# Second feed-forward: chunks 5, 6 and 9, 10 in pairs with seven block products, weight blocks summed by accumulating transfers

## The chip, the cores and the metric

The kernel runs on one core of one Trainium2 chip. The metric is the device time of one execution in microseconds; the time of a kernel is the median of several runs. Before the change it is 784.1 us, the median of three runs between 783.6 and 784.39.

The engines are named as in the profile: PE (TensorE) multiplies matrices and loads its stationary operand with LDWEIGHTS (PEld), DVE (VectorE) and ACT (ScalarE) work on tiles, POOL (GpSimd) and SP (SyncE) here mainly issue transfers.

## The reference

One layer of a streaming encoder over 256 positions and a model width of 1024: a feed-forward, a mixing block, a memory attention, and a second feed-forward. The change is in the second feed-forward alone:

```python
def rmsnorm(x, g):
    y = x32 * lax.rsqrt(jnp.mean(x32 * x32, axis=-1, keepdims=True) + EPS)
    return (y * g.astype(jnp.float32)).astype(x.dtype)

def swiglu(h, w_in, w_down):
    gate, up = jnp.split(h @ w_in, 2, axis=-1)
    return (jax.nn.silu(gate) * up) @ w_down
...
        h = rmsnorm(x, ffn2_pre_g[l])
        x = x + 0.5 * rmsnorm(swiglu(h, ffn2_w_in[l], ffn2_w_down[l]), ffn2_post_g[l])
```

`w_in` is 1024 x 5632 (gate and up), `w_down` 2816 x 1024, all in float32.

## The kernel before

**Arithmetic.** Each float32 operand of a product is split into a high part rounded to float32r and the rest, hi and lo (`split`, `load_split`). A product is hi·hi + hi·lo + lo·hi, three matmuls for a block of 128 rows of the inner dimension. The inputs are kept transposed (inner dimension on the partitions), hi and lo side by side, in `X`, of class `Joined`.

**Weights.** A unit is a tile of 128 x 1024 float32 (512 KB): two blocks of 128 rows and 512 columns. `load_split` loads it from SP into a `raw` buffer (4 of them), copies it to `hi` on ACT and subtracts on DVE for `lo` (8 buffers each). So a unit is split as soon as the unit eight places ahead of it has been used by PE, and loaded as soon as a raw buffer has been split.

**Chunks.** The hidden width 2816 is cut into 11 chunks of 256. A chunk's input projection has 512 columns (gate and up), that is 4 units: units 0 and 1 are the first half of the inner dimension, 2 and 3 the second.

- By tokens (`act_tok`, chunks 0 and 1 of the second feed-forward): the inputs of 128 tokens are stationary, 512 weight columns move, 24 matmuls of 128x512 for each half of the tokens. The result has tokens on the partitions; `act_evac` applies the gate, and `flush` transposes it on PE (4 transposes of 128x128 for a pair of token halves and a chunk) and splits it into `acts`.
- By columns (`act_col`, chunks 2 to 10): 128 weight columns are stationary, the tokens' hi and lo (512 wide) move; the lo weights take the hi tokens alone (256 wide). That is 32 matmuls of 128x512 and 32 of 128x256 for a chunk, and the result is already transposed. `added` sums the two halves of a PSUM bank, with a copy on ACT and an addition on DVE.
- Down-projection (`down`): chunk c, token half h, 2 units, 12 matmuls of 128x512 into one of two pairs of PSUM banks that accumulate over all chunks (`accs`).

**Order.** The loop over chunks does a chunk's input projection and behind it the down-projection of an earlier chunk: chunk 2 with down-projection 0, and so on to chunk 8 with 6; chunk 9 has none, chunk 10 is followed by 7. The last three (8, 9, 10) come at the end, first token half first, followed by `post` (norm, gain, residual, store). Each engine runs its queue strictly in order; a scheduler has placed the instructions of DVE, ACT, PE, POOL and SP in advance, and `high_priority`, `issue_after` and `after` steer it. PSUM has 4 banks for `acc`, 2 for `mm`, 2 for `tr`. The pool `extra` has 4 buffers of 128 x 1024.

Of the kernel before, what the change touches and what calls it, by code (L numbers as in the profile page):

```python
# [11 lines left out]
F32 = mybir.dt.float32  # L12
F32R = mybir.dt.float32r
# [5 lines left out]
P = 128  # L19
# [12 lines left out]
SETS = ((0, 1), (2, 4), (8, 16), (32,), (64,), (128,))  # L32

STAG = 3

L_ACT = 21
L_F1 = 24
# [41 lines left out]
def block_kernel(ctx: ExitStack, tc: tile.TileContext, wts, head_in, gf_in, x_in, mem_in, memT_in, cols, rows, fbias, masks, out):  # L79
# [12 lines left out]
    def MM(*args, **kw):  # L92
        log.append(PE.matmul(*args, **kw).ins)  # L93
# [9 lines left out]
    def nm(s):  # L103
        count[0] += 1
        return f"{s}_{count[0]}"

    def m4(shape, dt=F32, n="m"):
        return mp.tile(shape, dt, tag="m4", name=nm(n))

    def s1(n=1, dt=F32, name="s"):  # L110
        return sp.tile([P, n], dt, tag=f"s{n}", name=nm(name), bufs=16)

    def acc():
        return pp.tile([P, 512], F32, tag="acc", name=nm("acc"), bufs=4)

    def mm():
        return pp.tile([P, 512], F32, tag="mm", name=nm("mm"), bufs=2)
# [13 lines left out]
    def parts_of():  # L131
        return [wp.tile([P, D], F32R, tag=t, name=nm(t), bufs=8) for t in ("hi", "lo")]
# [15 lines left out]
    def unit(name, i):  # L148
        u = _AT[name] + i
        if u not in cache:  # L150
            cache[u] = load_split(wts[u - 4], behind=hold.get(u), parts=place.get(u))
        return cache[u]
# [4 lines left out]
    def blk(units, kb, n=512):  # L157
        hi, lo = units[kb // 2]
        o = (kb % 2) * 512
        return hi[:, o : o + n], lo[:, o : o + n]  # L160

    def split(hi, lo, src):
        a = S.copy(hi, src)
        b = V.tensor_tensor(out=lo, in0=src, in1=hi.bitcast(F32), op=ALU.subtract)
        return a.ins, b.ins

    class Pair:
# [7 lines left out]
        def more(self):  # L175
            self.h.append(m4([P, 4, T], F32R, "hT"))
            self.l.append(m4([P, 4, T], F32R, "lT"))
# [65 lines left out]
    def bc(a, shape, dim):  # L243
        return a.unsqueeze(dim).to_broadcast(shape)
# [172 lines left out]
    def ffn(w_in, w_dn, X, r2, n_tok, i_row, first_half, second_half=None):  # L417
# [7 lines left out]
        def flush(n):  # L425

            if late:
                c = late.pop(0)
                tr = trp()
                trv = tr.rearrange("p (j t) -> p j t", j=2)  # L430
                with after(n):
                    for h in range(2):
                        for j in range(2):
                            PE.transpose(trv[:, j, h * P : (h + 1) * P], ats[c, h][:, j * P : (j + 1) * P], ident)  # L434
                    split(acts[c][:, 0], acts[c][:, 1], trv)

        def act_evac(ps, c, h):
            sg = sp.tile([P, FC], F32, tag="c1", name=nm("sg"), bufs=7)
            S.activation(sg, ps[:, :FC], AF.Silu, scale=r2[h])
            a = sp.tile([P, FC], F32, tag="c1", name=nm("at"), bufs=7)  # L440
            V.tensor_tensor(out=a, in0=ps[:, FC:], in1=sg, op=ALU.mult)
            ats[c, h] = a
            if h == 1:
                late.append(c)

        def act_tok(c, h):
            ps = mm()
# [35 lines left out]
        def down(c, h, cols=((0, 512), (512, 1024))):  # L483
            act = acts[c]
            hs = slice(h * P, (h + 1) * P)
            for j in range(2):
                wh, wl = unit(w_dn, 2 * c + j)
                ah, al = act[:, 0, j, hs], act[:, 1, j, hs]
                for lo, up in cols:
                    for i, (a, w) in enumerate(((ah, wh), (ah, wl), (al, wh))):  # L490
                        MM(accs[h][lo // 512][:, lo % 512 : lo % 512 + up - lo], a, w[:, lo:up], start=(c == 0 and j == 0 and i == 0), stop=(c == NFF - 1 and j == 1 and i == 2))

        for c in range(n_tok):
            acts[c] = m4([P, 2, 2, T], F32R, "act")
        for h in range(2):
# [8 lines left out]
        if callable(r2):  # L504
# [6 lines left out]
                    act_evac(outs[c][h], c, h)  # L511
            n_tok = 2
        for c in range(n_tok, NFF):
            acts[c] = m4([P, 2, 2, T], F32R, "act")
            if c == 2 and first_half:
                n = len(log)
                (outs,) = act_first((c,), mm)
                for h in range(2):
                    flush(n + L_ACT + 24 * h)
                    act_evac(outs[h], c, h)  # L520
            else:
                n = len(log)
                up = act_col(c)
                flush(n + L_ACT)
                flush(n + L_ACT + 20)
                split(acts[c][:, 0], acts[c][:, 1], up)
            if c == 6:
                grow = load_row(i_row)
                if first_half:
                    with tc.issue_after(loads[-1]):  # L530
                        nc.sync.dma_start(masks_s, masks)
            if accs is None:
                accs = [[acc(), acc()], [acc(), acc()]]

            while done < (NFF - STAG if c == NFF - 1 else min(c - 1, NFF - STAG - 1)):
                n = len(log)
                for h in range(2):
                    down(done, h)
                flush(n + L_ACT)
                done += 1  # L540
        left, right = (0, 512), (512, 1024)
# [836 lines left out]
```

## Time and profile before

| | |
|---|---|
| median of three runs | 784.1 us |
| span of the profiled execution | 782.4 us |
| second feed-forward's chunk 3 begins, by PE's timeline | 631.5 us |
| chunks 9 and 10 begin | 731.2 and 742.4 us |
| last matmul ends | 775.5 us |
| HBM read, written | 146.24 MB, 1.06 MB |

The profiled execution's own time is the span; the difference to the median of the runs is what lies around it. The profile gives starts and durations for each instruction. A matmul's duration overlaps with the next one, so that its cost is read from the distance between starts. "Idle before" is time in which an engine stood waiting, with what released it.

### The profile page before, as it was taken

The page shows a single profiled execution, that of the slowest core. Times are in us where ns is not written, and L with a number is a line of the kernel's source. Part 1 is how long each engine was busy: PE and PEld are TensorE (multiplying, and loading weights), DVE is VectorE, ACT ScalarE, POOL GpSimd, SP SyncE. Part 2 cuts the span into 40 slices and gives each one's busy share as a digit, 9 for nine tenths or more (in the row PEclk, how much of TensorE's full clock was granted, in tenths as well). Part 3 has the DMA queues.
Part 4 walks back from the last instruction along what each step waited for, and adds up shares of the span by engine and source line. Part 5 has one row for each costly group of instructions (what it writes and reads, how often), then busy time and mean ns, then how long its engine had stood idle before and what let it go on. Part 6 is the DMA issues. An engine that isn't in the chain of part 4 may idle for free.

```text
span 782.4 us, 12131 instructions
## 1 busy us (share of the span) xinstructions
PE 773.8 (99%) x4598; PEld 667.2 (85%) x4598; DVE 560.1 (72%) x907; ACT 467.2 (60%) x789; POOL 16.0 (2%) x39
## 2 busy tenths in 40 slices
PE   9999999999999999999999999999999999999996
PEld 7888888888888998898888888888888888888885
DVE  6766655586778999888776666885588566655663
ACT  7664544566765668567686345753667655544542
POOL 0000000000000101100000000000000000000000
PEclk9999999999999999999999999999999999999999
DMA  9766665464654545835576655465175556665431
GB/s 346 258 218 205 226 210 207 162 214 141 218 187 145 181 137 178 303 105 167 196 271 220 212 186 166 152 203 182 54 268 163 168 181 208 208 208 192 162 108 54
DMA packets 44506, 148.09 MB, mean 189 GB/s; under 512 B 5144, under 2 KB 8864, under 8 KB 44448
## 3 DMA queue, kind: packets, MB, share of 16 engines
q1 hardware_dynamic: 43168, 144.83, 54.4%
q0 software_dynamic: 848, 2.12, 1.0%
q8 instruction: 36, 0.59, 0.3%
q10 hardware_dynamic: 432, 0.37, 0.1%
q14 instruction: 22, 0.18, 0.1%
HBM read 146.24 MB, written 1.06 MB: 188 GB/s over the span
## 4 chain that ended last, share of the span: by engine, by line
PE 98%; DMA 1%; DVE 0%; ACT 0%; issue 0%; SPq 0%; DVEq 0%; ACTq 0%
PE mm L93 43%; PE acc L93 39%; PE tr L93 14%; PE tr L375 1%; DMA head<-in_head_dram 1%; PE tr L1015 0%; PE tr L434 0%; PE tr L1109 0%; PE acc L1228 0%; DVE xs L411 0%; DVE post L406 0%; ACT hi L590 0%; SPq L574 0%; ACT hlT L362 0%; SPq L569 0%
## 5 line engine op out<-in xcount | busy, mean ns | idle before, releaser
L145 DVE TENSOR_TENSOR lo<-raw,hi 128x1024 fp32r<-128x1024 f32 (+1 forms) x252 | 299.4, 1203 | 70.2 <-ACT hi L143 48.0
L143 ACT CAST hi<-raw 128x1024 fp32r<-128x1024 f32 (+1 forms) x252 | 254.8, 1037 | 68.5 <-DMA raw<-in_wts_dram 32.2
L93 PE MATMUL mm<-hi,hlT 128*128 128x512 f32 (+1 forms) x480 | 143.3, 378 | 0.0
L93 PE MATMUL acc<-hi,act 128*128 128x512 f32 x352 | 111.2, 390 | 0.0
L93 PEld LDWEIGHTS mm<-hi,hlT 128*128 128x128 f32 x480 | 88.3, 188 | 14.3
L93 PE MATMUL mm<-hlT,hi 128*128 128x512 f32 (+1 forms) x384 | 91.8, 374 | 0.0
L93 PE MATMUL mm<-lo,hlT 128*128 128x512 f32 (+1 forms) x240 | 89.4, 378 | 0.0
L93 PEld LDWEIGHTS mm<-hlT,hi 128*128 128x128 f32 x384 | 68.5, 189 | 11.1
L93 PEld LDWEIGHTS acc<-hi,act 128*128 128x128 f32 x352 | 66.2, 188 | 13.4
L93 PE MATMUL tr<-hlT,hi 128*128 128x512 f32 x304 | 76.1, 392 | 0.0
L93 PE MATMUL acc<-lo,act 128*128 128x512 f32 x176 | 68.8, 391 | 0.0
L93 PE MATMUL acc<-hlT,hi 128*128 128x512 f32 x272 | 68.4, 393 | 0.0
L93 PEld LDWEIGHTS tr<-hlT,hi 128*128 128x128 f32 x304 | 54.7, 189 | 9.8
L93 PEld LDWEIGHTS acc<-hlT,hi 128*128 128x128 f32 x272 | 48.9, 189 | 8.8
L93 PE MATMUL mm<-hlT,lo 128*128 128x256 f32 x352 | 54.6, 283 | 0.0
L93 PEld LDWEIGHTS mm<-hlT,lo 128*128 128x128 f32 x352 | 50.0, 190 | 3.3
L93 PEld LDWEIGHTS mm<-lo,hlT 128*128 128x128 f32 x240 | 45.0, 188 | 6.9
L215 ACT COPY plo<-mm 128x256 f32<-128x256 f32 x40 | 14.9, 372 | 48.9 <-PE mm L93 48.9
L93 PEld LDWEIGHTS tr<-hlT,lo 128*128 128x128 f32 x304 | 41.5, 190 | 3.0
L93 PE MATMUL tr<-hlT,lo 128*128 128x256 f32 x304 | 42.4, 282 | 0.0
L93 PEld LDWEIGHTS acc<-hlT,lo 128*128 128x128 f32 x272 | 37.3, 190 | 2.7
L93 PE MATMUL acc<-hlT,lo 128*128 128x256 f32 x272 | 38.6, 283 | 0.0
(256 smaller groups left out, 1008.9 us busy)
## 6 DMA issues: line engine op xcount, KB each, us to landing
raw<-in_wts_dram SPq DMA_DIRECT2D x247, 512.0 KB, 4.4
raw<-in_gf_dram SPq DMA_DIRECT2D x12, 344.0 KB, 3.8
head<-in_head_dram SPq DMA_DIRECT2D x7, 392.0 KB, 6.7
grow<-in_rows_dram SPq DMA_DIRECT2D x4, 512.0 KB, 6.7
xs<-in_x_dram SPq DMA_DIRECT2D x2, 512.0 KB, 7.8
cbm<-cd POOLq DMA_DIRECT2D x2, 512.0 KB, 7.6
brow<-in_rows_dram SPq DMA_DIRECT2D x4, 256.0 KB, 4.0
memT<-in_memT_dram SPq DMA_DIRECT2D x2, 512.0 KB, 5.3
```

Source lines behind the costliest of these rows:

```text
L93: log.append(PE.matmul(*args, **kw).ins)
L143: S.copy(h, r)
L145: V.tensor_tensor(out=l, in0=r, in1=h.bitcast(F32), op=ALU.subtract)
L215: S.copy(lo, ps[:, T:])
L375: PE.transpose(blocks[-1][1], src(kb), ident)
```

## The change

`PAIRS` names chunks that are computed together with the next one: 5 with 6 and 9 with 10 in the second feed-forward, none in the first. A pair is a product of the inputs (two halves of tokens by two halves of the inner dimension) and of the weights (two halves of the inner dimension by two chunks), both seen as 2 x 2 blocks. Instead of the eight products of blocks that this takes by tokens, it is put together from seven, by a scheme of Strassen's kind (Winograd's form): some products take sums and differences of input blocks and sums of weight blocks, and the results are combined by additions.

- `pair_inputs`, once, at chunk 2: the sums and differences of the input blocks on DVE, then split. Since the second half of the tokens has another norm factor than the first, its inputs are scaled by the ratio (`rho`), and `q` takes it out again.
- `sum_load`, `more`: sums of weight blocks. The first summand is loaded from SP into a buffer of pool `extra`, each further summand is added by a transfer from POOL with `accum_op`. One sum ("sums") is used as W00 + W01 and then, with W11 added, again; the other ("both") as W01 + W11 and then, with W00 and W10 added, again. The third and fourth summands can be added only when the first version has been split.
- `act_pair`: the seven products, 12 matmuls of 128x512 each, with waiting down-projections put between them by `step_between`; then the combinations on DVE, four calls of `act_evac`, and transposes by `flush`.
- `act_evac` can multiply by `q` and by another scale.
- The loop over chunks takes a pair as one step.

On the engines, after scheduling: in PE's queue the first pair has the halves of down-projections 3 and 4 between its products, one each after the first and second product, after b3 and after b4, and twelve matmuls of chunk 7 ahead of the pair's last product (that of e). The second pair has four matmuls of b3 ahead of the second product, and eleven of down-projection 7 ahead of its last product. ACT copies the new "sums" (first unit) ahead of `S.copy(p1, b0)` in the second pair, behind it in the first. POOL has twenty new transfers, SP eight new ones and four fewer plain units.

```diff
--- before.py
+++ after.py
+
+PAIRS = {"f1_in": (), "f2_in": (5, 9)}
 ...
-        def act_evac(ps, c, h):
+        def act_evac(ps, c, h, r=None, q=None):
             sg = sp.tile([P, FC], F32, tag="c1", name=nm("sg"), bufs=7)
-            S.activation(sg, ps[:, :FC], AF.Silu, scale=r2[h])
+            silu = S.activation(sg, ps[:, :FC], AF.Silu, scale=r2[h] if r is None else r).ins
             a = sp.tile([P, FC], F32, tag="c1", name=nm("at"), bufs=7)
-            V.tensor_tensor(out=a, in0=ps[:, FC:], in1=sg, op=ALU.mult)
+            if q is None:
+                V.tensor_tensor(out=a, in0=ps[:, FC:], in1=sg, op=ALU.mult)
+            else:
+                V.scalar_tensor_tensor(out=a, in0=ps[:, FC:], scalar=q, in1=sg, op0=ALU.mult, op1=ALU.mult)
             ats[c, h] = a
             if h == 1:
                 late.append(c)
+            return silu
 ...
+        def pair_inputs():
+            rho = sp.tile([P, P], F32, tag="c1", name=nm("rho"), bufs=7)
+            V.reciprocal(rho, row[:, :P])
+            V.tensor_tensor(out=rho, in0=row[:, P:], in1=rho, op=ALU.mult)
+            q = s1(name="q")
+            V.reciprocal(q, r2[1])
+            V.tensor_tensor(out=q, in0=r2[0], in1=q, op=ALU.mult)
+            xf = [m4([P, 4, T], n="xf") for _ in range(2)]
+            for k in range(2):
+                for i in range(2):
+                    x = X.t[2 * k + i].bitcast(F32)
+                    V.tensor_tensor(out=xf[k][:, 2 * i : 2 * i + 2], in0=x[:, :, 0], in1=x[:, :, 1], op=ALU.add)
+                V.tensor_tensor(out=xf[k][:, :, P:], in0=xf[k][:, :, P:], in1=bc(rho, [P, 4, P], 1), op=ALU.mult)
+            a, b, d, e = (xf[k][:, :, h * P : h * P + P] for h in range(2) for k in range(2))
+            ss = [m4([P, 2, 4, P], n="ss") for _ in range(2)]
+            de, aed, ad, baed = (t[:, i] for t in ss for i in range(2))
+            V.tensor_tensor(out=de, in0=d, in1=e, op=ALU.subtract)
+            V.tensor_tensor(out=aed, in0=a, in1=de, op=ALU.subtract)
+            V.tensor_tensor(out=ad, in0=a, in1=d, op=ALU.subtract)
+            V.tensor_tensor(out=baed, in0=b, in1=aed, op=ALU.subtract)
+            out = {}
+            for n, x in (("baed", baed), ("aed", aed), ("de", de), ("ad", ad), ("e", e)):
+                t = m4([P, 2, 4, P], F32R, "sx")
+                split(t[:, 0], t[:, 1], x)
+                out[n] = t
+            return out, q
+
+        def sum_load(c, n, halves):
+            t = []
+            for j in range(2):
+                r = wp.tile([P, D], F32, tag="extra", name=nm("sraw"), bufs=4)
+                more(r, c, *halves[0], j, None)
+                more(r, c, *halves[1], j, ALU.add)
+                t.append(r)
+            return t
+
+        def more(r, c, k, n, j, op):
+            src = wts[_AT[w_in] + 4 * (c + n) + 2 * k + j - 4]
+            if op is None:
+                loads.append(nc.sync.dma_start(r, src).ins)
+            else:
+                G.dma_start(r, src, accum_op=op)
+
+        def act_pair(c, between):
+            sx, q = pairs_in
+
+            def of(n):
+                return lambda kk: (sx[n][:, 0, kk], sx[n][:, 1, kk])
+
+            def of_x(k):
 ...
+            def splits(t):
+                u = []
+                for r in t:
+                    p = parts_of()
+                    split(p[0], p[1], r)
+                    u.append(p)
+                return u
+
+            def plain(k, n):
+                return [unit(w_in, 4 * (c + n) + 2 * k + j) for j in range(2)]
+
+            def product(ps, stat, u, start):
+                for kk in range(4):
+                    ah, al = stat(kk)
+                    wh, wl = blk(u, kk)
+                    for i, (x, y) in enumerate(((ah, wh), (ah, wl), (al, wh))):
+                        MM(ps, x, y, start=start and kk == 0 and i == 0, stop=kk == 3 and i == 2, skip_group_check=not start)
+
+            def step_between():
+                if between:
+                    between.pop(0)()
+
+            def half_tile(n):
+                return sp.tile([P, 512], F32, tag="z2", name=nm(n), bufs=3)
+
+            sums, both = sums_of_pair.pop(c)
+            b0 = mm()
+            product(b0, of_x(0), plain(0, 0), True)
+            vw = m4([P, 2, 512], n="vw")
+            pc = m4([P, 2, 512], n="pc")
+            p1, v, w = pc[:, 0], vw[:, 0], vw[:, 1]
+            S.copy(p1, b0)
+            step_between()
+            product(b0, of_x(1), plain(1, 0), False)
+            act_evac(b0, c, 0)
+            step_between()
+            b3 = mm()
+            u = splits(sums)
+            for j in range(2):
+                more(sums[j], c, 1, 1, j, ALU.add)
+            product(b3, of("de"), u, True)
+            step_between()
+            b4 = mm()
+            u = splits(both)
+            for k, n in ((0, 0), (1, 0)):
+                for j in range(2):
+                    more(both[j], c, k, n, j, ALU.add)
+            product(b4, of("ad"), u, True)
+            step_between()
+            b1 = trp()
+            product(b1, of("aed"), splits(sums), True)
+            with tc.high_priority():
+                V.tensor_tensor(out=v, in0=p1, in1=b1, op=ALU.subtract)
+                V.tensor_tensor(out=w, in0=b3, in1=v, op=ALU.subtract)
+                t = half_tile("c11")
+                V.tensor_tensor(out=t, in0=w, in1=b4, op=ALU.subtract)
+                act_evac(t, c + 1, 1, r2[0], q)
+            b2 = trp()
+            product(b2, of("baed"), plain(1, 1), True)
+            with tc.high_priority():
+                t = half_tile("c01")
+                V.tensor_tensor(out=t, in0=w, in1=b2, op=ALU.add)
+                act_evac(t, c + 1, 0)
+            step_between()
+            product(b4, of("e"), splits(both), False)
+            t = half_tile("c10")
+            V.tensor_tensor(out=t, in0=v, in1=b4, op=ALU.add)
+            silu = act_evac(t, c, 1, r2[0], q)
+            if c + 1 == NFF - 1:
+                table(silu)
+            while between:
+                step_between()
+
+        def pair_loads(c):
+            if c in pairs and c not in sums_of_pair:
+                sums_of_pair[c] = sum_load(c, 0, ((0, 0), (0, 1))), sum_load(c, 1, ((0, 1), (1, 1)))
+
+        sums_of_pair = {}
+        pairs, pairs_in = PAIRS[w_in], None
 ...
         for c in range(n_tok, NFF):
+            if c - 1 in pairs:
+                continue
+            if c > 2 and c not in pairs:
+                pair_loads(c + 1)
+            if c in pairs:
+                pair_loads(c)
             acts[c] = m4([P, 2, 2, T], F32R, "act")
-            if c == 2 and first_half:
+            if c in pairs:
+                acts[c + 1] = m4([P, 2, 2, T], F32R, "act")
+                downs = [(i, h) for i in range(done, min(c, NFF - STAG - 1)) for h in range(2)]
+                done = max(done, min(c, NFF - STAG - 1))
+
+                def one(i, h):
+                    n = len(log)
+                    down(i, h)
+                    if h == 1:
+                        flush(n + L_ACT - 12)
+
+                act_pair(c, [lambda i=i, h=h: one(i, h) for i, h in downs])
+            elif c == 2 and first_half:
 ...
-            if c == 6:
+            last = c + 1 if c in pairs else c
+            if c <= 6 <= last:
 ...
-
-            while done < (NFF - STAG if c == NFF - 1 else min(c - 1, NFF - STAG - 1)):
+            if c == 2 and pairs:
+                pairs_in = pair_inputs()
+
+            while done < (NFF - STAG if last == NFF - 1 else min(c - 1, NFF - STAG - 1)):
                 n = len(log)
                 for h in range(2):
                     down(done, h)
+                    if last > c:
+                        flush(n + 11)
+                        n = len(log)
                 flush(n + L_ACT)
                 done += 1
```

1 line of the change is left out of this document (added).

## The prediction

> **What bounds the kernel now.** I read the page's summary first, then its chain of waits, then the stretches of the second feed-forward by engine, and last the order of instructions there.
>
> ```profile
> span 782.4 us, 12131 instructions
> PE 773.8 (99%) x4598; PEld 667.2 (85%) x4598; DVE 560.1 (72%) x907; ACT 467.2 (60%) x789; POOL 16.0 (2%) x39
> PE 98%; DMA 1%; DVE 0%; ACT 0%; issue 0%; SPq 0%; DVEq 0%; ACTq 0%
> 681.37:697.99 16.62, 16.62 (x90) 14.34 (x89) 10.50 (x14) 8.54 (x13) 0.00 (x0) 1.00 0.55 193
> 714.60:731.21 16.61, 16.61 (x89) 14.34 (x88) 10.77 (x15) 8.91 (x13) 0.00 (x0) 1.00 0.56 199
> 731.21:753.53 22.32, 22.32 (x129) 19.66 (x128) 12.95 (x19) 12.16 (x20) 0.00 (x0) 1.00 0.57 189
> 753.53:782.40 28.87, 21.95 (x98) 17.84 (x96) 12.69 (x24) 7.80 (x19) 0.00 (x0) 0.94 0.11 37
> ```
>
> The chain that ended last is 98% PE, and in the last four rows (length; then PE, PEld, DVE, ACT, POOL busy; granted clock; DMA share; GB/s) PE never pauses before its last matmul at 775. So a PE microsecond saved or lost inside the stage moves the end. DVE is busy 10.5 of 16.6 us, the DMA engines 0.55 to 0.57 of the time. The stretches are chunk 6 (681.37), chunk 8 (714.60) and chunks 9 and 10 (731.21).
>
> **The change part by part.** *Products.* Pitches, from starts in PE's timeline:
>
> ```profile
> 614.05 1.98 PE L93 MATMUL mm<-hlT,hi 128*128 128x512 f32 x8
> 618.21 0.60 PE L434 MATMUL tr<-ident,at 128*128 128x128 f32 x4
> 626.07 0.40 PE L93 MATMUL acc<-hi,act 128*128 128x512 f32 x1
> ...
> 681.37 1.98 PE L93 MATMUL mm<-hlT,hi 128*128 128x512 f32 x8
> 692.52 0.40 PE L93 MATMUL acc<-hi,act 128*128 128x512 f32 x1
> 697.99 1.98 PE L93 MATMUL mm<-hlT,hi 128*128 128x512 f32 x8
> ```
>
> A chunk by columns takes 692.52 − 681.37 = 11.15 us; the 24 matmuls of a down-projection that follow take 5.47 us, 0.228 each. Two chunks: 22.30 us. A pair has 7 products of 12 matmuls of that same shape, 84 × 0.228 = 19.15 us. A pair must also transpose its activations, eight times, which columns don't need. Chunk 2 has eight such transposes among its matmuls and takes 626.07 − 614.05 = 12.02 us, so they cost 0.87 us. Net 22.30 − 19.15 − 0.87 = 2.28 us a pair, **4.6 us for both**, if PE never waits.
>
> *Vector work.* A pair splits 14 weight blocks instead of 8, and evacuates with five 512-wide and four 256-wide operations in place of the sums and the gate of two chunks. The inputs' sums (some 15 operations 512 wide) are made once, during chunks 2 and 3.
>
> ```profile
> L145 DVE TENSOR_TENSOR lo<-raw,hi 128x1024 fp32r<-128x1024 f32 x57 | 68.7, 1220 | 20.8 <-ACT hi L143 12.8 <-PE tr L93 7.8 <-ACT hlT L362 0.2
> L143 ACT CAST hi<-raw 128x1024 fp32r<-128x1024 f32 x57 | 58.0, 1049 | 11.1 <-DMA raw<-in_wts_dram 7.9 <-PE mm L93 2.3
> L466 DVE TENSOR_TENSOR up<-up,gate 128x512 f32<-128x512 f32 x9 | 6.2, 684 | 0.0
> L217 DVE TENSOR_TENSOR gate<-mm,plo 128x256 f32<-128x256 f32 x18 | 7.6, 422 | 17.5 <-ACT plo L215 17.5
> L163 ACT CAST act<-up 128x512 fp32r<-128x512 f32 x9 | 5.6, 622 | 15.9 <-DVE up L466 15.9
> ```
>
> Inputs: 15 × 0.68 = 10 us of DVE, against 16.6 − 10.5 = 6 us idle in each of two chunk periods: hidden, because what is pushed back there are down-projection blocks and the next chunk's first two blocks, split some 12 us ahead of use; 0 taken, 2 us if that lead is short. Pair: 14 splits of 1.14 us pitch (below) plus 5 us make 21 us against PE's 19.15 us (ACT: 14 × 1.05 and some 4 us of evacuations) and the down-projections among it. That fits on average; where it doesn't is a matter of waits.
>
> *Transfers.* A pair loads 6 plain blocks and 4 first summands from SP, and adds 10 further summands from POOL: 20 transfers of 512 KB instead of 8. No accumulating transfer is in the trace. Call X the time from its issue to its landing.
>
> ```profile
> q1 hardware_dynamic: 43168, 144.83, 54.4%
> raw<-in_wts_dram SPq DMA_DIRECT2D x247, 512.0 KB, 4.4
> cbm<-cd POOLq DMA_DIRECT2D x2, 512.0 KB, 7.6
> out_dram<-xs SPq DMA_DIRECT2D x1, 128.0 KB, 1.8
> rd<-runs POOLq DMA_DIRECT2D x4, 1.0 KB, 2.1
> DMA to landing us min/median/max: 3.2/4.5/7.6
> SPq L141 <- DVE lo L145: 85.7, 30, 8.5
> ```
>
> Bounds: 3.2 us (the fastest plain block of this stage, last row but one) and 7.6 us (a plain block from POOL, one row broadcast) + 1.5 us for reading the destination too (512 KB at 144.83 MB / (0.544 × 782.4 us) = 340 GB/s), 9.1 us. I take 4.7 us: the plain block's median plus the 0.3 us by which POOL's smallest transfer lands later than a small one of SP's. That says the destination's read hides beside that of HBM.
>
> On all 16 engines a plain block occupies 1.5 us by the row above. The Trainium skill (Collectives: The Full Stack, "The bandwidth ceiling: the fold count and why AG ≠ RS ≠ AR") says that an adding transfer is slow "because the add needs **two source reads**", half the rate of a copy; by it the block would occupy 3.1 us and X be 6.2, which by the sum below gives 784.9 us and, with transfers queueing, the slow rival. No run so far has such a transfer.
>
> *First pair* (PE starts it where chunk 5 starts, T0 = 664.76). Four half down-projections lie between its products, so PE reaches the end of the sixth product at 10 × 2.73 = 27.3 us. ACT and DVE are strict queues here. The second operand ("both") is read by 13.4 us, when its buffers come free at 9.6 and 10.9; then two summands go in one behind the other, each waiting for the one before: landed at 13.4 + 2X. Behind that wait ACT still copies 1.05 us of it and 1.05 us of chunk 7's first block, which PE wants at 27.3. Wait: 15.5 + 2X − 27.3 = **2X − 11.8**; at 4.7, none. The other sum has ten microseconds to spare. SP's next first summand waits for the same landing, with down-projection 5 and chunk 8 queued behind it; PE needs those some 15 us later.
>
> *Second pair* (T0 where chunk 9 starts). No down-projection is left to lie between its products but the one of chunk 7, 24 matmuls near the end. The splits just before it are as in the row pattern before chunk 9:
>
> ```profile
> 725.28 2.36 DVE L145 TENSOR_TENSOR lo<-raw,hi 128x1024 fp32r<-128x1024 f32 x2 [1.30 <-PE tr L93]
> 727.90 1.21 DVE L145 TENSOR_TENSOR lo<-raw,hi 128x1024 fp32r<-128x1024 f32 x1
> 729.63 1.22 DVE L145 TENSOR_TENSOR lo<-raw,hi 128x1024 fp32r<-128x1024 f32 x1
> 730.77 0.68 DVE L164 TENSOR_TENSOR act<-up,act 128x512 fp32r<-128x512 f32 x1
> 731.37 1.22 DVE L145 TENSOR_TENSOR lo<-raw,hi 128x1024 fp32r<-128x1024 f32 x1
> ```
>
> These become: two plain blocks, both halves of "sums", the activation, the first half of "both". (Pitch: 730.77 − 729.63 = 1.14 us a split, 0.6 for 512-wide work.) So POOL may add to the first half of sums at T0 − 2.1, and to the halves of both at T0 + 1.4 and + 2.5.
> First wait: on ACT the copy of the first sum's new half stands ahead of the copy of the first product, which PE waits for before the second product, at T0 + 3.65. Ready at −2.1 + X + 1.05 + 0.65. Wait X − 4.05, which the second wait contains.
> Second wait: both lands at 2.5 + 2X. DVE then has eight splits and six smaller steps in order (8 × 1.14 + 4 × 0.6 + 2 × 0.33 = 12.2 us) before the activation that PE transposes after 99 matmuls, at T0 + 22.5. Ready at 14.9 + 2X: **wait 2X − 7.6**, 1.8 us at 4.7. Behind it are the last weight blocks (SP waits for those splits to give raw buffers back, as in the last row above) and the last down-projections.
>
> Sum at X = 4.7: 782.4 − 4.6 + 0 + 1.8 = 779.6 us of span. The median of the runs, 784.1, lies 1.7 above the span, which stays: **781.3 us**.
>
> **The rivals.** As X decides: the waits are 0 below 3.8 and eat the gain of 4.6 at X = 6.0.
>
> 1. *Slower: adding costs the DMA engines twice, and the six transfers of pair two queue up.* From T0 − 0.9 on they follow each other at 3.1 us: the sixth lands at −0.9 + 6 × 3.1 + 0.5 = 18.2 instead of 11.9, wait 1.8 + 6.3 = 8.1 us; in pair one, with four plain blocks (6 us) between, some 2 us. 782.4 − 4.6 + 8.1 + 2 + 1.7 = **789.6 us**. It decides from X = 6.4 on (+1.6 us). For: 20 transfers instead of 8 in a stage at 0.55, POOL's 512 KB rows of 7.6. Against: those rows are broadcasts, and DMA is idle 0.45 of the time.
> 2. *Break-even*, X from 5.3 to 6.4, half of the destination's read showing: **784 us**.
> 3. *Full gain*: X up to 4.2, adding costs nothing over the fastest plain block. 784.1 − 4.6 = **779.5**, at most 780.3. For: DMA is near idle at pair two's end. The Trainium skill (DMA: Bandwidth & Descriptors, "Anatomy of one DMA — SWDGE (gpsimd) path") fits 2.0 us + bytes/436e3, an estimate of 3.2 us for 512 KB, the trace's own minimum; the sum by it is 779.5 us. Against: six of them overlap.
> 4. *DVE becomes the bound in pair two even without the transfers*: from T0 on its work up to that activation is 14 × 1.14 + 4 × 0.6 + 3 × 0.33 = 19.4 us, less than 22.5; a lower granted clock after a wait (0.94 in the last row of the first view, behind idle time) would add 1 to 3 us: **786**.
>
> **How the numbers follow.** Forecast, X from 4.2 to 5.3: 0.36. Full gain 0.08. Break-even 0.18. Queueing transfers 0.30, the fourth 0.08. A difference of 0.2% (1.6 us) is what can be told from no change: faster 0.44, same 0.18, slower 0.38. The forecast's own range is 780.3 to 782.5 (waits of 0.8 and 3.0 us at X = 4.2 and 5.3). The range goes from full gain to rival 1 with a microsecond for pair one: 779.5 to 791; X = 9.1 would be 784.1 − 4.6 + 10.6 + 6.4 = 796.5, left out.
>
> **What would show it.** PE's starts: the pair's products at 0.228 us a matmul and 84 of them a pair; else the 4.6 is wrong. The accumulating groups' time to landing is X itself: 4.2 to 5.3 supports me, above 6.4 the first rival. Idle time of PE: none in pair one; in pair two under 1 us at the second product and about 2 us before the transposes at its end. Most of it should be released by DVE, behind an ACT copy that waited for a summed block. If PE waits during chunks 3 and 4, the inputs' sums weren't hidden. I am wrong if second summands land later than about 12 us after POOL could send the first.

## The result: 815.25 us, and the profile after

| | before | after |
|---|---|---|
| median of four runs each, on the same chip | 784.08 us (783.6 to 784.39) | 815.25 us (814.3 to 818.92) |
| ratio, 95% interval | | 1.0404 (1.0390 to 1.0419) |
| span of the profiled execution | 782.4 us | 817.1 us |

The forecast was 781.3 us, faster; the kernel is 31 us slower, above the range of 779.5 to 791. The page of the changed kernel, the lines that answer to those shown of before:

```profile
span 817.1 us, 12083 instructions
PE 785.7 (96%) x4526; PEld 670.2 (82%) x4526; DVE 581.9 (71%) x932; ACT 477.8 (58%) x796; POOL 33.3 (4%) x59
q1 hardware_dynamic: 43744, 146.93, 51.1%
q0 software_dynamic: 3728, 12.61, 7.8%
issue 49%; PE 41%; DMA 7%; DVE 1%; POOL 1%; ACT 0%; DVEq 0%; POOLq 0%; ACTq 0%
sraw<-in_wts_dram POOLq DMA_DIRECT2D x20, 512.0 KB, 9.0
```

PE has fallen from 99% to 96% of a longer span. In the chain of waits PE has 41% instead of 98%, DMA 7% instead of 1%; for 49% ("issue") the profile shows no cause of a wait. The 20 adding transfers take 9.0 us from issue to landing in the median, not 4.7. The engines' working time of POOL's queue (q0) rose from 1.0% to 7.8%.

What PE waited for in the second feed-forward of the changed kernel (in total, times, longest, in us):

```profile
PE tr L95 <- DVE vw L610: 9.3, 1, 9.3
PE acc L95 <- DVE up L219: 3.9, 1, 3.9
PE mm L95 <- DVE c L624: 2.8, 1, 2.8
PE acc L95 <- ACT hi L145: 2.7, 1, 2.7
PE mm L95 <- ACT pc L589: 2.7, 1, 2.7
PE acc L95 <- DVE lo L147: 0.9, 1, 0.9
```

With two of 0.6 and 0.5 us that is 23.4 us. DVE is named most often, but DVE had been waiting itself. The stretches of the same execution (columns as in the prediction):

```profile
615.00:631.50 16.50, 14.29 (x81) 12.02 (x79) 8.21 (x11) 6.03 (x11) 0.00 (x0) 1.00 1.05 281
671.58:698.55 26.97, 26.97 (x120) 22.34 (x119) 13.23 (x13) 11.95 (x14) 6.93 (x8) 1.00 1.00 267
698.55:708.23 9.68, 0.39 (x3) 0.03 (x1) 6.60 (x7) 4.83 (x5) 0.07 (x1) 0.78 1.06 275
708.23:714.10 5.87, 5.76 (x13) 3.95 (x14) 3.77 (x5) 2.42 (x3) 1.66 (x2) 0.50 1.01 352
754.34:780.00 25.66, 19.24 (x75) 14.91 (x74) 11.74 (x12) 10.94 (x14) 4.26 (x5) 0.91 0.80 164
780.00:810.24 30.24, 29.67 (x115) 23.13 (x114) 17.50 (x27) 11.92 (x22) 0.00 (x0) 0.85 0.25 88
...
671.58:754.34 82.76, 70.55 (x317) 57.84 (x316) 48.72 (x57) 39.16 (x51) 9.62 (x12) 0.90 0.81 239
```

Two things are to be seen. The DMA engines stand at a share of 1.0 ahead of chunk 3 and all through the first pair, 671.6 to 714.1, while DVE and ACT are half idle. And behind each long wait the granted clock is 0.50 for a while (fourth row), so that a wait can cost more than its length; in the rows from 754.34 and from 780.00 it is 0.91 and 0.85.

Below, a kernel's loss is read off PE's timeline in three parts: how much later than before it starts chunk 5 or the first pair (664.76 us), how much longer it takes from there to the start of chunk 9 or the second pair (66.45 us), and from there to the end of the last matmul (44.27 us).

| kernel | median, us | lead | first pair's period | from chunk 9 on |
|---|---|---|---|---|
| changed kernel | 815.25 | +6.8 | +16.3 | +11.6 |
| e1, first pair alone | 799.94 | +4.2 | +9.8 | 0.0 |
| e2, no adds | 783.57 | +1.1 | +0.2 | −1.9 |
| e3, input sums alone | 784.29 | −0.2 | 0.0 | 0.0 |
| e4, plain transfers for adds | 797.89 | +1.5 | +7.0 | +4.7 |
| e5, adds early and unread | 805.54 | +10.8 | +10.8 | −1.8 |
| e6, narrow adds | 783.76 | +1.1 | +0.5 | −1.1 |
| e7, part of the wait filled | 815.01 | +6.8 | +16.9 | +11.2 |
| e8, GpSimd adds | 804.20 | −0.2 | +8.5 | +10.8 |
| e9, unread adds in place | 814.57 | +7.2 | +16.8 | +6.3 |
| e10, first adds later | 817.50 | +0.3 | +20.4 | +11.3 |
| e11, VectorE adds | 791.62 | −0.4 | +2.1 | +4.9 |
| e12, VectorE adds, last pair alone | 790.06 | +0.8 | 0.0 | +5.8 |
| e13, nothing to sum | 787.63 | +1.0 | +0.4 | +0.2 |
| e14, sums made early | 791.99 | +4.2 | +4.2 | +0.4 |
| e15, whole wait filled | 817.20 | +8.5 | +15.1 | +10.0 |

The parts are from the one profiled execution of each, the medians from all runs; the kernel before came to 784.1 to 785.0 us beside them. The changed kernel, e7 and e15 are the same program up to the first pair but for one small tile, and their lead goes from 6.8 to 8.5 us: where much is lost, 2 us between two kernels mean little.

### The profile page after: what moved, and what is told of

Same layout as the page of the kernel before. It is cut to its first block, busy times and chain, and to the rows that moved or that the text cites. A ratio compares the mean times of both kernels' runs of the same rounds, so it can differ in the third digit from the quotient of the medians.

```text
span 817.1 us, 12083 instructions
## 1 busy us (share of the span) xinstructions
PE 785.7 (96%) x4526; PEld 670.2 (82%) x4526; DVE 581.9 (71%) x932; ACT 477.8 (58%) x796; POOL 33.3 (4%) x59
## 3 DMA queue, kind: packets, MB, share of 16 engines
HBM read 158.82 MB, written 1.06 MB: 196 GB/s over the span
## 4 chain that ended last, share of the span: by engine, by line
issue 49%; PE 41%; DMA 7%; DVE 1%; POOL 1%; ACT 0%; DVEq 0%; POOLq 0%; ACTq 0%
PE acc L95 19%; PE mm L95 15%; PE tr L95 7%; DMA sraw<-in_wts_dram 5%; DMA cbm<-cd 1%; POOL sraw L547 1%; DVE lo L147 1%; DMA raw<-in_wts_dram 0%; DMA rd<-runs 0%; PE tr L436 0%; ACT hi L165 0%; POOL cbm L1138 0%; PE tr L377 0%; DVE xs L413 0%; DVE post L408 0%
## 5 line engine op out<-in xcount | busy, mean ns | idle before, releaser
L95 PE MATMUL mm<-hi,hlT 128*128 128x512 f32 (+1 forms) x512 | 155.1, 381 | 2.7 <-ACT pc L589 2.7
L95 PE MATMUL mm<-hlT,hi 128*128 128x512 f32 (+1 forms) x320 | 80.5, 385 | 3.3 <-DVE c L624 2.8
L95 PEld LDWEIGHTS mm<-hlT,hi 128*128 128x128 f32 x320 | 59.4, 198 | 13.9 <-DVE c L624 3.2
L95 PE MATMUL tr<-hlT,hi 128*128 128x512 f32 x240 | 61.5, 397 | 9.3 <-DVE vw L610 9.3
L95 PEld LDWEIGHTS tr<-hlT,hi 128*128 128x128 f32 x240 | 43.5, 191 | 17.4 <-issue 9.7
L95 PE MATMUL mm<-hlT,lo 128*128 128x256 f32 x288 | 46.5, 287 | 0.0
L95 PEld LDWEIGHTS mm<-hlT,lo 128*128 128x128 f32 x288 | 42.1, 194 | 2.8
L166 DVE TENSOR_TENSOR lo<-sraw,hi 128x1024 fp32r<-128x1024 f32 x16 | 19.4, 1223 | 30.2 <-ACT hi L165 30.0
L95 PEld LDWEIGHTS acc<-lo,act 128*128 128x128 f32 x176 | 34.1, 194 | 7.8 <-DVE lo L147 1.3
L165 ACT CAST hi<-sraw 128x1024 fp32r<-128x1024 f32 x16 | 16.6, 1048 | 31.7 <-DMA sraw<-in_wts_dram 27.4
```

## The experiments

The theory to be tried (A): the adding transfers are to blame. Its rivals: the vector work and the order of the queues (B), and POOL's queue whatever it carries (C). A itself has two forms: PE waits for summed blocks that land late (A1), or the traffic delays the plain weight blocks (A2).

### The first four: one pair, no adds, the input sums, plain transfers

e1 takes one pair, e2 drops the adds, e3 keeps the input sums only, e4 turns adds into plain transfers:

```diff
-PAIRS = {"f1_in": (), "f2_in": (5, 9)}
+PAIRS = {"f1_in": (), "f2_in": (5,)}
...
-                G.dma_start(r, src, accum_op=op)
+                pass
...
-            if c == 2 and pairs:
+            if c == 2 and w_in == "f2_in":
...
-                G.dma_start(r, src, accum_op=op)
+                G.dma_start(r, src)
```

> Only chunks 5, 6 are a pair; 9 and 10 are column chunks as before. Theory A (adding transfers land late and crowd the DMA engines, each pair pays where its own transfers run): the trace of the changed kernel starts the second pair 754.34 - 731.21 = 23.1 us late, so about 784 + 23 = 807 us, and from chunk 9 on nothing more is lost. Rival B (input sums on VectorE and the longer vector queue cost most): the sums stay and so does their part, 6 to 7 us ahead of the pair, but the pair itself costs little: 788 to 793 us.

Measured: 799.94 us (797.67 to 805.16), ratio 1.0202 (1.0161 to 1.0244), between the two. The first pair alone loses 9.8 us in its period, with the second pair present 16.3. What the changed kernel has in that period besides are the second pair's first loads and first adds; what each of them adds is not shown.

> Leaves out every adding transfer, so the summed blocks hold only their first summand; all matmuls, vector work and first loads stay. Theory A: no late landing is left, the six block gain shows: 784 - 4.6 = 779.5 us, up to 782 with small waits. Rival B (vector work, queue order, input sums): little changes against the changed kernel, 800 us or more.

Measured: 783.57 us, ratio 0.9990 (0.9976 to 1.0003). So the adds are the whole loss, and vector work and queue order (B) are not. But the gain is missing as well: PE still waits 3.1 us (same view as above):

```profile
PE mm L95 <- DVE at L444: 1.4, 1, 1.4
PE mm L95 <- DVE c L624: 1.2, 1, 1.2
PE mm L95 <- DVE c L613: 0.5, 1, 0.5
```

The first is ahead of chunk 3, where SP's queue now has four first summands between the weights. The other two are PE's matmuls into a PSUM bank of pool `mm` whose content DVE has yet to combine (`c`). In the second pair, where nothing of a next chunk needs those banks, 1.9 of the 2.28 us do show.

> No pairs, only the sums of the stationary inputs and their splitting are computed (nobody reads them). Theory A: hidden behind chunks 2 and 3, 784 to 785 us. Rival B: the stall ahead of chunk 3 of the changed kernel (3.9 us and the clock drop after it, 6.8 us by the start of chunk 4) comes from the 10 us of sums on VectorE: 788 to 791 us.

Measured: 784.29 us, ratio 0.9998 (0.9989 to 1.0007). Hidden, as theory A had it; the stall ahead of chunk 3 isn't theirs.

> Each adding transfer becomes a plain transfer to the same place from the same queue, so a summed block holds only its last summand; instructions and order are those of the changed kernel. Theory A in the form that the addition is what costs (its packets take the DMA engines 1.9 times as long for each MB as those of the plain queue): landing falls from 9.0 to under 6 us and most of the loss goes, 780 to 790 us. Rival C (it is GpSimd's queue and its waits, whatever the transfer does): landing stays near 9 us and the time near 815 us.

Measured: 797.89 us, ratio 1.0172 (1.0148 to 1.0196), between A and C, and so is the landing with a median of 6.9 us: the same bytes without the addition cost 14 us, the addition another 17. What a transfer costs the engines can be read from the view of the DMA queues between 672 and 712 us (packets, MB, share of 16 engines; then issues with the median to landing), first of the changed kernel, then of e4:

```profile
q0 software_dynamic: 1152, 4.19, 55.6%
q1 hardware_dynamic: 1913, 6.95, 45.3%
...
sraw<-in_wts_dram POOLq DMA_DIRECT2D x10, 512.0 KB, 8.9
raw<-in_wts_dram SPq DMA_DIRECT2D x9, 512.0 KB, 8.0
```

```profile
q1 hardware_dynamic: 2281, 8.33, 58.0%
q0 software_dynamic: 1378, 4.99, 33.6%
...
sraw<-in_wts_dram POOLq DMA_DIRECT2D x8, 512.0 KB, 7.0
```

An MB of adding transfers takes 0.556 × 40 / 4.19 = 5.3 us of all 16 engines, an MB of SP's plain ones 0.453 × 40 / 6.95 = 2.6; in e4 POOL's plain transfers take 0.336 × 40 / 4.99 = 2.7. So the queue is not at fault, the addition doubles a transfer's work: 2.8 us for a block of 0.524 MB instead of 1.4. The Trainium skill has this rule for the adding step of a collective (Collectives: The Full Stack, "The bandwidth ceiling: the fold count and why AG ≠ RS ≠ AR"; the prediction cited it and set it aside): two source reads, half the rate. The trace agrees in the rate, 5.3 to 2.6. And the plain blocks beside them land after 8.0 us, against 4.4 before.

### Waiting for sums, or waiting for weights

In the changed kernel it looks as if the late sums hold PE up. ACT's timeline (start, duration, the idle time before it and what ended it):

```profile
697.50 1.05 ACT L165 CAST hi<-sraw 128x1024 fp32r<-128x1024 f32 x1 [10.56 <-DMA sraw<-in_wts_dram]
701.77 1.04 ACT L165 CAST hi<-sraw 128x1024 fp32r<-128x1024 f32 x1 [3.23 <-DMA sraw<-in_wts_dram]
702.73 3.88 ACT L145 CAST hi<-raw 128x1024 fp32r<-128x1024 f32 x4
```

That reading is tested by splitting another tile in place of the sums, so that ACT and DVE don't wait for a sum's landing:

```diff
-                    split(p[0], p[1], r)
+                    pace[j] = split(p[0], p[1], xs[:, j])[1]
```

> All transfers of the changed kernel run, in their order and each add behind the split it waited for, but the summed blocks are split from another tile that is ready long before, so the products use wrong weights and nobody waits for an add to land. Theory A1 (what costs is waiting for landings, the copies of the summed blocks holding up ScalarE and VectorE): back to the level without adds, 783 to 787 us. Rival A2 (what costs is the traffic: the adds keep the DMA engines busy, and the plain weight loads of the neighbouring chunks land late): 800 us or more. A sum of both would lie between, and the stall ahead of chunk 3 alone (no summed block is waited for there) should stay under both.

Measured: 805.54 us, ratio 1.0273 (1.0256 to 1.0290): A2. But the run is not quite what its text says. The order asked for (`issue_after`) did not hold the adds behind the splits: POOL sent the six later adds of the first pair at 625 to 650 us instead of 674 to 693. So they fell on chunk 4, where PE lost 5.7 us to late weights, and the second pair, whose adds had also gone out ahead, lost nothing. The cost went where the traffic went.

Yet e5 is the cleanest test of A2. No wait for a summed tile is left in it, neither ACT's (27.4 us in the changed kernel, between 600 and 800 us) nor SP's (12.1 us there; SP waits when a first summand is to go into a tile to which an add is still under way). Even so the first pair's ten adds cost 10.8 us ahead of that pair, and the second pair's ten, which here all fall into the first pair's period, 10.8 us again (without adds, in e2, these parts are 1.1 and 0.2). e9 holds the adds in their place by a real dependency, added to the transfer:

```diff
-                    G.dma_start(r, src, accum_op=op)
+                    i = G.dma_start(r, src, accum_op=op).ins
+                if behind:
+                    tc.add_manual_dep(i, behind.name, mybir.DependencyInfo(mybir.DependencyClass.Sync, mybir.DependencyReason.DATA), reason="held")
```

> The run with unread adds, repeated with each later add really held until the split of its tile has been done (in the earlier run the adds went out as soon as the first ones had landed, some 30 to 60 us ahead of the place they have in the changed kernel). Products again use a tile that is ready, nobody waits for a landing. Theory A2 (traffic alone): the first pair, with the weights of chunks 7 and 8 to be loaded beside it, still loses 10 us or more, and the time is above 798 us. Theory A1 (waits for landings): 783 to 790 us. The second pair has only the last down blocks to load beside it: there both expect that little is lost once nobody waits for a landing.

Measured: 814.57 us, ratio 1.0366 (1.0332 to 1.0399), the time of the changed kernel, though ACT and DVE wait for no sum. ACT's timeline in e9 shows what stands in its place:

```profile
701.64 1.05 ACT L145 CAST hi<-raw 128x1024 fp32r<-128x1024 f32 x1 [2.47 <-DMA raw<-in_wts_dram]
711.42 1.04 ACT L145 CAST hi<-raw 128x1024 fp32r<-128x1024 f32 x1 [8.74 <-DMA raw<-in_wts_dram]
```

The plain blocks come late, sums or not. In the first pair's period e9 loses 16.8 us, the changed kernel 16.3. But that is not traffic alone, since SP still waits for landings (20.7 us, four times). SP's timeline in e9 (start, time from the first to the end of the last issue):

```profile
686.77 1.69 SPq L143 DMA_DIRECT2D raw<-in_wts_dram  x2
699.38 3.42 SPq L548 DMA_DIRECT2D sraw<-in_wts_dram  x2
702.90 0.87 SPq L143 DMA_DIRECT2D raw<-in_wts_dram  x2
```

SP issues nothing from 688.5 to 699.4. The block for which ACT waits until 711.42 is issued at 702.90, behind two of the second pair's first summands, though DVE had split two `raw` buffers by 696.25. So a part of the 16.8 us can be order in SP's queue, and e9 does not show how much; e5 has no such wait. From chunk 9 on e9 loses 6.3 against 11.6: there I had expected little, and some 5 us go with the engines' waits for landings.

### Fewer bytes, other places

e6 narrows the adds; e10 holds the first four adds of the first pair by a dependency like that of e9, on the last matmul traced ahead of chunk 4:

```diff
-                G.dma_start(r, src, accum_op=op)
+                G.dma_start(r[:, :64], src[:, :64], accum_op=op)
...
-                more(r, c, *halves[1], j, ALU.add)
+                more(r, c, *halves[1], j, ALU.add, log[-1] if c == 5 else None)
```

> Adds move 64 of the 1024 columns only (the other columns keep the first summand), so a sixteenth of the bytes; waits and order as in the changed kernel. If the cost goes with the bytes (engines' time), landing falls to 2 to 4 us and the time to 783 to 788 us. If it is a fixed price of issuing, of the queue and of completion, landing stays above 6 us and the time above 800 us.

Measured: 783.76 us, ratio 0.9982 (0.9972 to 0.9992), as without adds, with a landing of 3.1 us: no fixed price of issuing or queueing is left, the cost goes with the bytes.

> The changed kernel, with the first four adds of the first pair held until the matmuls ahead of chunk 4 are done (at 648 instead of 611 us); nothing else is moved. If the stall ahead of chunk 3 comes from these four adds, it goes, and chunk 4 starts where it did without adds, 649 instead of 655 us; the sums still land ahead of their first use. Then 809 us if nothing else changes, about 815 us if the bytes collide with the loads of chunks 5 and 7 instead.

Measured: 817.50 us, ratio 1.0417 (1.0391 to 1.0444). The stall ahead of chunk 3 is gone (chunk 4 starts at 648.5 us), so it was theirs. And it is paid in the pair instead, by PE's timeline in e10:

```profile
677.14 0.79 PE L95 MATMUL mm<-hi,hlT 128*128 128x512 f32 x1 [6.47 <-ACT pc L591]
```

In the changed kernel this matmul starts at 677.02. The work for the DMA engines is the same, and at 648 us it costs as much as at 611.

### Adding on an engine

If the transfers are the trouble, the blocks can be loaded once and added in SBUF, by GpSimd (e8) or VectorE (e11, e12: `V` for `G`). The product of the fourth block stands earlier, and each sum has a product's time to be formed:

```diff
+            def add(out, a, b):
+                for j in range(2):
+                    G.tensor_tensor(out=out[j], in0=a[j], in1=b[j], op=ALU.add)
...
+            add(sums, r00, both)
+            add(both, both, r11)
+            add(sums, sums, r11)
+            add(both, sums, r10)
```

> Both pairs with no adding transfer: every block is loaded once, and GpSimd adds the tiles, 8 adds of 128x1024 for each pair; the products come in another order (the fourth output's product ahead of the sums that need a second addition). If the forecast's gain was right and only the transport of the sums was wrong: 784.1 - 4.6 = 779.5 us, up to 782 us with small waits. Rival: GpSimd's adds come late or slow VectorE down, or the pair's VectorE chain holds the PSUM banks of chunk 7 as it did without adds: 783 to 792 us.

Measured: 804.20 us, ratio 1.0251 (1.0235 to 1.0267): slower, as the rival had it, but 12 us beyond its range. DVE's timeline in e8, without and with GpSimd's adds beside it (these begin at 651.96 and 654.75 and take 2.54 and 3.09 us):

```profile
649.88 2.35 DVE L147 TENSOR_TENSOR lo<-raw,hi 128x1024 fp32r<-128x1024 f32 x2
...
652.90 6.02 DVE L166 TENSOR_TENSOR lo<-raw,hi 128x1024 fp32r<-128x1024 f32 x2 [0.33 <-ACT hi L165]
```

Each stands for two instructions: two splits take 2.35 us alone and 6.02 beside the adds. The Trainium skill (SBUF — State Buffer, "Who interferes with whom") has it so: a VectorE instruction with two SBUF inputs and a GpSimd instruction that reads SBUF exclude each other for their whole length. The rows agree that the splits wait; for how long at a time they don't show.

> Both pairs without adding transfers, in the order of the run with GpSimd's adds, but VectorE adds the tiles (8 adds of 128x1024 for each pair; a split of that size takes it 1.22 us, so 9.8 us for each pair) and the second x block's weights are asked for earlier. If GpSimd's 3 us adds, and the splits beside them that took 3.2 instead of 1.22 us, made that run slow: 780 to 783 us. If VectorE in its order is too late for the products: 786 to 795 us.

> The same for chunks 9, 10 alone, with chunks 5 and 6 as column chunks. Half of the gain if it is there: 784.1 - 2.3 = 782 us; if the adds on VectorE are late, 785 to 790 us.

Measured: 791.62 us, ratio 1.0092 (1.0075 to 1.0109), and 790.06 us, 1.0069 (1.0054 to 1.0084). The rival again. In the last pair VectorE is late, and then the clock takes as much again. PE's timeline in e12, and then its stretches before and after that wait:

```profile
751.71 0.71 PE L95 MATMUL mm<-hi,sx 128*128 128x512 f32 x1 [2.50 <-DVE c L616]
```

```profile
731.97:749.20 17.23, 16.78 (x73) 13.25 (x71) 14.60 (x16) 8.15 (x10) 0.00 (x0) 1.00 0.17 62
752.92:758.90 5.98, 5.98 (x15) 4.68 (x16) 3.33 (x5) 3.19 (x4) 0.00 (x0) 0.53 0.26 88
```

VectorE is busy 14.6 of 17.2 us, and the next 6 us of matmuls run at a clock of 0.53: 5.98 × (1 − 0.53) = 2.8 us more.

### The ceiling, and sums made ahead

e13 puts a plain block in the place of each sum; e14 builds the sums in DRAM during the stages before (the lines are e14's; in e13 `made` loads a plain block):

```diff
+            def made(n):
+                return [load_split(wsum[c, n][j]) for j in range(2)]
...
+        d = (G.dma_start(to, of, accum_op=op, max_dma_last_dim=1024) if op else G.dma_start(to, of, max_dma_last_dim=1024)).ins
...
+        if todo and len(log) >= 600 and (len(log) - 600) % 85 == 0:
+            early_sum()
```

> Both pairs in the order of the runs with GpSimd's and VectorE's adds, but a plain weight block stands in the place of each sum (wrong weights in four of the seven products): 14 plain loads for each pair, no addition of weights anywhere, nothing but SP's ordinary queue. If the forecast's product arithmetic holds and only the sums were in the way: 784.1 - 4.6 = 779.5 us, up to 781 us. If the pair's own chain on VectorE and the PSUM banks take the gain back, as in the run without adds: 783 to 785 us.

Measured: 787.63 us, ratio 1.0036 (1.0023 to 1.0050), above both. With 14 plain blocks for a pair, ready in time, the pairs' periods are as long as before (+0.4 and +0.2 in the table). The waits within them:

```profile
PE mm L112 <- DVE c L608: 1.0, 2, 0.5
PE mm L112 <- ACT pc L586: 0.9, 2, 0.6
PE tr L455 <- DVE at L463: 0.9, 1, 0.9
```

PE waits for banks and activations that DVE's combinations and ACT's copy of the first product (`pc`) have yet to give, about 3 us of the 4.6. These rows are of an execution of 786.6 us, the twelve runs go from 785.1 to 791.0; what the longer ones lost stays open.

> The same kernel with the right sums: 16 copies and 16 adding transfers of 512 KB build them in DRAM ahead of time, one every 85 matmuls (about 14 us) during the earlier stages, and the pairs load them as plain blocks. If traffic costs only where the DMA engines are full (share 1.0) and is free where they are at 0.4 to 0.6: within 1 us of the run with nothing to sum, faster than before. If each add costs half of its engines' time wherever it runs (20 adds of 2.8 us cost 31 us in the changed kernel): 16 x 2.8 + 16 x 1.4 = 67 us of engines' time, 810 us or more.

Measured: 791.99 us, ratio 1.0096 (1.0081 to 1.0111): 4.4 us above the run with nothing to sum, and no 810. Two long stretches of the earlier stages in e14, and its POOL queue:

```profile
100.00:330.00 230.00, 227.73 (x1780) 200.77 (x1779) 177.44 (x289) 147.80 (x247) 21.25 (x37) 1.00 0.70 215
330.00:560.00 230.00, 228.67 (x1194) 195.24 (x1193) 167.72 (x296) 135.94 (x251) 15.36 (x20) 1.00 0.69 217
```

```profile
q0 software_dynamic: 11600, 18.90, 11.1%
```

POOL's queue took 0.111 × 791.5 − 0.010 × 782.4 = 80 us more of the engines than before, and cost 4.4; the 20 adds of the changed kernel took 0.078 × 817.1 − 0.010 × 782.4 = 56 us and cost 31. Added traffic costs where the engines are full, here at 1.0, and little where they stand at 0.7. The sums of e14 are made in DRAM and not in SBUF, though, so the two kinds of adds need not be alike. And in the executions traced e14's first pair has a period 3.8 us longer than e13's, with no adding transfer in it; why stays open.

### The clock

e7 and e15 put 28 and 44 matmuls by a zero block into the first pair's long wait:

```diff
+            for i in range(28 if c == 5 else 0):
+                MM(b4, zero, blk(us, i % 4)[0], start=False, stop=False, skip_group_check=True)
```

> The changed kernel with 28 matmuls by a zero block (they add nothing) between two products of the first pair, 28 x 0.228 = 6.4 us of work that nothing waits on otherwise. If a wait costs its own length only, filling it changes nothing: 815 us. If the granted clock, which falls to 0.50 after the 9.3 us wait and stays there with 6 us of matmuls running, costs another 3 us, the filled kernel is faster by 2 to 4 us although it does more: 811 to 813 us.

> As the run with the filled wait, with 44 matmuls by a zero block (10.0 us) instead of 28 (6.4 us). If the clock falls because PE stands still, it stays at 1.00 until 714 us and the pair's last product takes 2.7 instead of 5 us; then, if the clock is a cost of its own, 811 to 813 us. If chunk 7's weights are late anyway and set the time, PE only waits longer behind it: 814 to 817 us.

Measured: 815.01 us (813.3 to 818.9) and 817.20 us (815.9 to 818.1). In e7 4.1 us of the wait were left, and the clock fell all the same, so it decides nothing. In e15 it stays up:

```profile
698.00:711.00 13.00, 12.77 (x57) 10.21 (x55) 6.90 (x8) 6.17 (x7) 0.61 (x1) 1.00 1.04 273
711.00:716.00 5.00, 5.00 (x24) 4.17 (x25) 4.29 (x5) 1.40 (x2) 1.72 (x2) 1.00 0.98 277
716.00:730.00 14.00, 9.33 (x46) 7.54 (x46) 6.79 (x10) 6.19 (x10) 0.00 (x0) 0.88 0.92 284
```

The pair's last product runs at full speed, and PE stands that much longer for the weights behind it, 4.7 us from 716 to 730. The second pair starts at 754.8 us, in the changed kernel at 754.3; the first pair's period is 1.2 us shorter, and the median no better. So in that period the lost clock costs little of its own: the blocks that land late set the pace.

## Why the prediction was wrong, point by point

**Products: right.** 84 matmuls a pair at 0.228 us; in the changed kernel the first six products and four half down-projections take 27.0 us to the start of their last matmul without a pause (second of the stretches above), 27.3 were forecast. **"If PE never waits": wrong**, even with nothing to sum. The prediction didn't follow which PSUM banks the next chunk's matmuls and the pair's own transposes need from DVE's combinations. Of 4.6 us the runs without adds show 0.7 (e2) or none (e13).

**Input sums hidden: right** (e3).

**X, the landing of an add: wrong**, and with it the forecast. Taken 4.7 from bounds of 3.2 to 9.1; measured 9.0 in the median of the 20 and 5.5 at the least. The step was "That says the destination's read hides beside that of HBM". It does not hide: an adding transfer takes the engines twice the time of a plain one (5.3 to 2.6 us per MB). The other page of the Trainium skill cited there (DMA: Bandwidth & Descriptors, "Anatomy of one DMA — SWDGE (gpsimd) path") led to an estimate of 3.2 us, below the fastest add's 5.5 us.

**The waits 2X − 11.8 and 2X − 7.6: the wrong model.** At 9.0 they give 6.2 and 10.4 us, with the gain 784.1 − 4.6 + 16.6 = 796.1 in all, 19 us short. (The 14.9 in the second wait should be 2.5 + 12.2 = 14.7, which changes nothing.) The prediction costed an add as a latency that only its reader waits for. e5 takes those waits away and still loses 10.8 us for each ten adds, ahead of the first pair and in its period: what counts first is the time for which the DMA engines are busy. Before, they were idle for 0.43 × 66.45 = 28.6 us of that period (first row), and busy in bursts (second row, tenths in slices of 1 us from 672 to 712):

```profile
664.76:731.21 66.45, 66.45 (x353) 57.35 (x352) 41.78 (x53) 34.16 (x49) 0.00 (x0) 1.00 0.57 196
...
DMA  0000019798999795100000699997999995100007
```

Ten adds of 2.8 us take 28 of it, and eight of the ten are issued within 23 us. Each plain block that then comes late stops ACT, DVE and PE in turn.

The prediction also saw that "SP's next first summand waits for the same landing", with plain weights queued behind it, and put it at nothing. In the changed kernel SP stands for 12.1 us so, 8.5 of them at once. Of the 31 us, e5 shows some 20 as traffic, with the adds in another place. How the rest divides between SP's queue, ACT's waits for sums and the place of the adds stays open.

**Rival 1 had the mechanism and the wrong size: 789.6.** It doubled the engines' work for the six transfers of the second pair, and gave 2 us to the first and none to chunk 3. Measured are 11.6 us from chunk 9 on, 16.3 in the first pair's period and 6.8 ahead of it. Its "against", the DMA engines idle 0.45 of the time, was the slip: an average over a stage in which SP's loads wait for raw buffers says nothing of the 40 us in which the adds must run. The price of the engines' time stood in the prediction, 3.1 us a block by the Trainium skill's two source reads; it was multiplied by six instead of twenty, and not laid beside the plain loads.

**Rival 4's clock** was there (0.50 behind every long wait), in the first pair with little effect (e15). In e12, where the DMA engines are at 0.26, it came with 2.8 us.

## What to carry to other kernels

Cost a transfer by the time that it keeps the DMA engines busy, an adding one twice, and add it up over the stretch in which it must run, beside the plain loads of that stretch; a latency per transfer is only the cost when the engines have room. Look, too, at what stands behind a waiting transfer in the queue that issues it. A mean share of 0.57 is no room if the loads come in bursts that fill the engines already. And when a wait is named for one tile, take that tile away and look whether another wait has its place: here the sums were read as the cause, and the plain weights came late without them.

## What the runs showed of the hardware that was not expected

- An adding transfer takes the DMA engines 5.3 us per MB, a plain one 2.6 to 2.7, from either queue; HBM reads rose only by the blocks' own bytes (146.24 to 158.82 MB, 24 blocks of 0.524 MB).
- The granted clock fell to about 0.5 after a wait of 2.5 us (e12), and lasted 6 us with matmuls running. The Trainium skill (TensorE: Matmul & The Clock Gate, "What's actually happening") gives about 3.4 us of idling for it, in windows that run freely; here less was enough.
- GpSimd needs 2.5 to 3.4 us to add two tiles of 128x1024, and a VectorE split beside it up to 3 us instead of 1.2 (e8).
